# Low parts of 24 weight tiles stored in the first half of a decoder block and loaded again in the second

## The chip, the cores and the metric

One Trainium2 chip, one core of it. The metric is the device time of one execution in microseconds (us); of several runs the median is given. TensorE (PE in the profile), VectorE (DVE), ScalarE (ACT), GpSimd (POOL) and SyncE (SP) each run their own instructions in order; SP, ACT and POOL also issue DMAs.

## The reference

A decoder block on x (1 x 1024 x 1024, float32), one layer. Cut to what matters here:

```python
h = modulate(rms_norm(x, norm1_w), shift1, scale1)
proj = einsum('btd,de->bte', h, w_in)              # 1024 x 7184
q, k, v, r, a_lr, su, sv, g_a, g_b = split(proj)
...                                                # gated linear attention on q, k, v; spatial gating on su, sv
merged = sigmoid(g_a) * o_gla + sigmoid(g_b) * o_sgu
x = x + gate1 * einsum('bte,ed->btd', merged, w_out)
h2 = modulate(rms_norm(x, norm2_w), shift2, scale2)
x = x + gate2 * peer(h2, peer_w_q, keys1, keys2, expert_down, expert_up)   # top-16 product keys, gathered experts
out = rms_norm(x, final_norm_w)
```

The three large products (w_in, w_out, peer_w_q) are dense; `peer` picks 128 experts for each token out of 16384 and gathers their rows.

## The kernel before

**Halves.** The 1024 tokens are worked on in two halves of 512 (`hf` 0 and 1). In each half the activations lie transposed in on-chip memory, and all dense products of the block are made for this half, so every weight is read from DRAM once in each half.

**High and low parts.** A float32 product is made of three matmuls in the fast format `F32R`: each operand is split into a high part, which is the value rounded to that format, and a low part, which is what remains. The products high x high, high x low and low x high are summed in PSUM (`mm3`, `mm3s`, lines 175 to 189). `hTh` and `hTl` are the two parts of the activations, `wh` and `wl` those of a weight tile.

**Weight tiles.** A tile is 128 x 512 float32, 256 KB. `plan` lists the tiles of both halves in the order of use: in each half 14 groups of `w_inp` with 8 tiles each (`order_`: V0, V1, QK0, QK1, SV0, SV1, R0, ...), 32 tiles of `w_outp` and 40 of `w_qp`, 184 in all, so 368 in the program. `weights_ahead(n)` takes tiles from the plan until n are made: SP issues the load into `wt` (4 buffers, `WT`; L1250), ScalarE copies it to `wh` (L1253), VectorE subtracts `wl = wt - wh` (L1254); `wh` and `wl` have 4 buffers each (`WS`). `stream` calls it with `LOOK + 1`, so that three tiles beyond the one in use are made. `group` multiplies one group's 8 tiles with the 512 tokens, 12 matmuls per tile, into four PSUM banks, and then an `ev_...` function empties them: `ev_v` on ScalarE (L1316), `ev_qk` on VectorE (L1382 to L1402) with factors that ScalarE computes.

**What else runs there.** In the first half the rows of the adaLN modulation are made from `w_ada` beside the groups (`ada_row`, loads on SP at L1103, sums on VectorE at L1106 and L1108). In the second half the best expert of each head, for the four token blocks of the first half, is worked off beside the groups (`direct_rows`): POOL gathers a row of `down` and of `up` for each token (L752, 512 KB each), VectorE forms the dot product (L764), ScalarE the GELU (L766), VectorE adds the weighted row to `yd` (L773). The routing of the first half's tokens also runs there (`route`, `pack_half`, `rare`: many small VectorE instructions; `rare` gathers scores `qsc` with an index `qix`, L422 and L428). After the attention of the second half the stream of the other experts begins (`peer_stream`), which runs to the end of the program.

**Order.** The code is traced without loops on the chip, and `TileContext(nc, schedule_with_timeline_sim=True)` then orders each engine's instructions by a planned timeline: an instruction stands where the plan has it ready, with the order of tracing as its priority. `tc.issue_after(x)` holds an instruction behind x. On the chip each engine goes through its instructions strictly in that order and waits on semaphores. A buffer of a pool is given again when all that read or write it are done; that wait falls on the instruction that writes it next.

Of the kernel before, what the change touches and what calls it, by code (L numbers as in the profile page):

```python
# [7 lines left out]
F32 = mybir.dt.float32  # L8
F32R = mybir.dt.float32r
# [3 lines left out]
OP = mybir.AluOpType  # L13
# [4 lines left out]
P = 128  # L18
D = 1024
KD = D // P  # L20
SEQ = 1024
HALF = 512
NHALF = SEQ // HALF
# [23 lines left out]
WT = 4  # L47
# [23 lines left out]
DIR = 4  # L71
RR = .5
RA = 1.0
NEG = -3.0e38
TINY = 1.1754944e-38

# [4 lines left out]
def block_kernel(ctx: ExitStack, tc: tile.TileContext, x, xT, cT, w_ada, b_ada, b_adaT, n1T, w_inp, w_alr,  # L81
                 w_al, b_alT, gla_w, ln_w, ln_b, wsT, sgu_bT, w_outp, n2_w, w_qp, keysT, tab, down, up, fin_w,
                 out, dbg=None):
    nc = tc.nc
# [3 lines left out]
    dram = ctx.enter_context(tc.tile_pool(name="dram", bufs=1, space=DRAM))  # L88
# [53 lines left out]
    s_g = [dram.tile([len(bs), P, PH * 2 * NK], F32, name=f"s_d{g}") for g, bs in enumerate(GROUPS)]  # L142
    yr_d = [dram.tile([P, D], F32, name=f"yr_d{g}") for g in range(NG)]
    y_d = [dram.tile([P, D], F32, name=f"y_d{b}") for b in range(BH)]
    ncs_of = [NCS] * NBLK + [TOPK] * NG
    tsh_d = [dram.tile([P, BH, 5 * NCS + 2], F32, name=f"tsh_d{i}") for i in range(NHALF)]
    ts_d = [tsh_d[b // BH][:, b % BH] for b in range(NBLK)]
# [55 lines left out]
    def tops16(v, ix, st):  # L203
        nc.vector.max(v[:, 0:8], st)
        nc.vector.max_index(ix[:, 0:8], v[:, 0:8], st)
        nc.vector.match_replace(st, v[:, 0:8], st, NEG)
        nc.vector.max(v[:, 8:16], st)
# [834 lines left out]
    qa, qr, qp, qdir, qm, qf = Queue(), Queue(), Queue(), Queue(), Queue(), Queue()  # L1042
    rate = {"a": 1.0, "r": RA, "d": RD, "p": RP, "m": 1.0}

# [8 lines left out]
    with ExitStack() as pa:  # L1053
        wst_p = pa.enter_context(tc.tile_pool(name="wstage", bufs=WT))
        wsp = pa.enter_context(tc.tile_pool(name="wsplit", bufs=WS))
# [184 lines left out]
        plan, made, last_wt = [], [], []  # L1240
        for _ in range(NHALF):
            plan += [(w_inp[g], k) for g in order_ for k in range(KD)]
            plan += [(w_outp[m], k) for _ in range(2) for k in range(KD) for m in range(2)]
            plan += [(w_qp[q], k) for q in (0, 0, 1, 2, 3) for k in range(KD)]

        def weights_ahead(n):
            while plan and len(made) < n:
                src, k = plan.pop(0)
                wt = wst_p.tile([P, 512], F32, name="wt")
                last_wt[:] = [nc.sync.dma_start(wt, src[:, k, :]).ins]  # L1250
                wh = wsp.tile([P, 512], F32R, name="wh")
                wl = wsp.tile([P, 512], F32R, name="wl")
                nc.scalar.activation(wh, wt, AF.Identity)  # L1253
                nc.vector.tensor_tensor(wl, wt, wh.bitcast(F32), op=OP.subtract)  # L1254
                made.append((wh, wl))

        for hf in range(NHALF):
# [6 lines left out]
            def stream(srcs, body, evac, pre=None, npsum=4, post=None):  # L1264
                pss = [mm.tile([P, 512], F32, name="mm", tag="mm") for _ in range(npsum)]
                for k in range(KD):
                    if pre:
                        pre(k)
                    weights_ahead(len(srcs) if pre else LOOK + 1)
                    ws = [made.pop(0) for _ in srcs]  # L1270
                    body(k, ws, pss)
                    if post and k in post:
                        post[k]()
                    step()
                for i in range(npsum):
                    evac(i, pss[i])
# [485 lines left out]
```

## Time and profile before

| | |
|---|---|
| median of 3 runs | 1452.01 us (1451.76 to 1453.45) |
| the profiled execution, its own time | 1450.17 us |
| its span, first to last instruction | 1448.4 us |
| mean granted TensorE clock | 0.971 |
| DMA moved, mean rate over the span | 345.00 MB, 238 GB/s |
| loads of `wt` from `w_inp` | 224, median 3.5 us from issue to landing |
| ScalarE copy `wh<-wt` | 368, mean 628 ns |
| VectorE subtract `wl<-wt,wh` | 368, mean 685 ns |

The rows of the profile that the text below shows are of these kinds. A group of instructions: line, engine, operation, output and inputs by the program's names, shape and count, then busy us and mean ns of one, then the idle time of the engine just before them and what ended it. A wait: who waited for whom, total us, times, longest. A timeline row: start in us from the span's start, duration, engine, line, operation, names, count, and in brackets the engine's idle time before it and what ended that. A stretch: its bounds and length, the busy time of each engine with the count of instructions, the granted TensorE clock, the mean share of the 16 DMA engines that were busy, and GB/s. Matmuls are pipelined, so their durations overlap: the spacing of the starts, not the duration, is what one costs.

### The profile page before, as it was taken

The page shows a single profiled execution, that of the slowest core. Times are in us where ns is not written, and L with a number is a line of the kernel's source. Part 1 is how long each engine was busy: PE and PEld are TensorE (multiplying, and loading weights), DVE is VectorE, ACT ScalarE, POOL GpSimd, SP SyncE. Part 2 cuts the span into 40 slices and gives each one's busy share as a digit, 9 for nine tenths or more (in the row PEclk, how much of TensorE's full clock was granted, in tenths as well). Part 3 has the DMA queues.
Part 4 walks back from the last instruction along what each step waited for, and adds up shares of the span by engine and source line. Part 5 has one row for each costly group of instructions (what it writes and reads, how often), then busy time and mean ns, then how long its engine had stood idle before and what let it go on. Part 6 is the DMA issues. An engine that isn't in the chain of part 4 may idle for free.

```text
span 1448.4 us, 19642 instructions
## 1 busy us (share of the span) xinstructions
PE 1348.1 (93%) x6004; PEld 1039.6 (72%) x6004; DVE 1091.7 (75%) x3114; ACT 737.9 (51%) x1611; POOL 278.7 (19%) x275
## 2 busy tenths in 40 slices
PE   3999999999999889997989999999988999789996
PEld 2778877888888778776868787887766886445553
DVE  6584768443468669988879888778889877799775
ACT  4454333333255456474534677556645555556542
POOL 0100001000000011422442133221111024443331
PEclk8899999999999999998999999999998999999999
DMA  9552454322258484757587689796687669987984
GB/s 321 184 214 95 170 184 161 105 95 88 88 171 280 160 291 168 265 177 275 194 308 263 222 325 343 286 354 216 219 324 264 227 216 356 355 347 303 419 331 166
DMA packets 120836, 345.00 MB, mean 238 GB/s; under 512 B 15033, under 2 KB 24505, under 8 KB 108690
## 3 DMA queue, kind: packets, MB, share of 16 engines
q0 software_dynamic: 32064, 165.95, 30.7%
q1 hardware_dynamic: 70992, 133.20, 26.8%
q10 hardware_dynamic: 17666, 44.53, 8.5%
q8 instruction: 48, 0.79, 0.2%
q14 instruction: 66, 0.54, 0.1%
HBM read 319.40 MB, written 24.23 MB: 237 GB/s over the span
## 4 chain that ended last, share of the span: by engine, by line
PE 41%; DMA 8%; DVE 7%; issue 5%; ACT 4%; POOL 1%; ACTq 0%; DVEq 0%; POOLq 0%
PE acc L606 7%; PE mm L181 6%; PE mm L182 6%; PE mm L184 6%; DMA uv<-in_tab_dram,ix 4%; PE mm L187 3%; PE mm L188 3%; PE mm L189 3%; PE aux L1655 2%; PE hps L578 1%; DMA wt<-in_w_inp_dram 1%; PE hps L579 1%; DVE wl L1254 1%; DVE uv L580 1%; DMA xb<-in_x_dram 1%
## 5 line engine op out<-in xcount | busy, mean ns | idle before, releaser
L1253 ACT ACTIVATE wh<-wt 128x512 fp32r<-128x512 f32 x368 | 228.2, 628 | 322.9 <-PE mm L182 133.5
L1254 DVE TENSOR_TENSOR wl<-wt,wh 128x512 fp32r<-128x512 f32 x368 | 247.7, 685 | 137.1 <-ACT wh L1253 73.2
L181 PE MATMUL mm<-wh,hTh 128*128 128x512 f32 x672 | 265.9, 398 | 3.1 <-ACT wh L1253 3.1
L182 PE MATMUL mm<-wh,hTl 128*128 128x512 f32 x672 | 263.8, 395 | 0.0
L184 PE MATMUL mm<-wl,hTh 128*128 128x512 f32 x672 | 207.6, 394 | 0.0
L181 PEld LDWEIGHTS mm<-wh,hTh 128*128 128x128 f32 x672 | 127.1, 189 | 35.0 <-ACT wh L1253 4.8
L182 PEld LDWEIGHTS mm<-wh,hTl 128*128 128x128 f32 x672 | 126.9, 189 | 27.1 <-issue 1.0
L184 PEld LDWEIGHTS mm<-wl,hTh 128*128 128x128 f32 x672 | 125.6, 188 | 27.0 <-DVE wl L1254 0.6
L525 POOL DMA_INDIRECT uv<-in_tab_dram,ix x74 | 80.4, 1086 | 262.9 <-ACT ix L557 178.3
L187 PE MATMUL mm<-wh,hTh 128*128 128x512 f32 x224 | 90.5, 413 | 8.4 <-ACT hTh L1211 5.5
L182 PE MATMUL mm<-hTl,wh 128*128 128x512 f32 x240 | 96.5, 402 | 0.0
L181 PE MATMUL mm<-hTh,wh 128*128 128x512 f32 x240 | 95.9, 400 | 0.0
L580 DVE SCALAR_TENSOR_TENSOR uv<-uv,hps 128x512 f32<-128x512 f32 x112 | 74.8, 679 | 24.5 <-DMA uv<-in_tab_dram,ix 16.8
L188 PE MATMUL mm<-wl,hTh 128*128 128x512 f32 x224 | 89.1, 398 | 0.1
L189 PE MATMUL mm<-wh,hTl 128*128 128x512 f32 x224 | 88.4, 397 | 0.0
L187 PE MATMUL mm<-hTh,wh 128*128 128x256 f32 (+1 forms) x208 | 71.6, 346 | 10.7 <-DVE q L1383 7.6
L188 PE MATMUL mm<-hTl,wh 128*128 128x256 f32 (+1 forms) x208 | 69.8, 337 | 3.0 <-DVE hTl L173 3.0
L184 PE MATMUL mm<-hTh,wl 128*128 128x512 f32 x240 | 71.4, 398 | 0.0
L752 POOL DMA_INDIRECT uvd<-in_down_dram,dix x32 | 37.1, 1159 | 177.8 <-DVE cidx L353 40.0
L618 DVE SCALAR_TENSOR_TENSOR vl<-uv,r,vh 128x512 fp32r<-128x512 f32 x84 | 61.3, 745 | 10.6 <-ACT vh L617 7.7
L189 PE MATMUL mm<-hTh,wl 128*128 128x256 f32 (+1 forms) x208 | 68.9, 337 | 0.0
L578 PE MATMUL hps<-hh,E 128*128 128x512 f32 x132 | 62.4, 473 | 4.5 <-DVE uv L580 3.6
(938 smaller groups left out, 2875.3 us busy)
## 6 DMA issues: line engine op xcount, KB each, us to landing
wt<-in_w_inp_dram SPq DMA_DIRECT2D x224, 256.0 KB, 3.5
wt<-in_w_qp_dram SPq DMA_DIRECT2D x80, 256.0 KB, 3.0
wada<-in_w_ada_dram SPq DMA_DIRECT2D x32, 512.0 KB, 4.8
wt<-in_w_outp_dram SPq DMA_DIRECT2D x64, 256.0 KB, 3.5
wada<-in_w_ada_dram SPq DMA_DIRECT2D x32, 256.0 KB, 5.8
s_d<-so ACTq DMA_DIRECT2D x28, 256.0 KB, 5.3
xr<-in_x_dram ACTq DMA_DIRECT2D x8, 512.0 KB, 6.5
x_d<-x ACTq DMA_DIRECT2D x8, 512.0 KB, 4.4
```

What stands on the lines that cost most here:

```text
L181: nc.tensor.matmul(ps, lh, rh, start=False, stop=False)
L182: nc.tensor.matmul(ps, *((lh, rl) if feat else (ll, rh)), start=False, stop=False)
L184: nc.tensor.matmul(ps, *((ll, rh) if feat else (lh, rl)), start=False, stop=False)
L187: nc.tensor.matmul(ps, lh, rh, start=first, stop=False)
L188: nc.tensor.matmul(ps, lh, rl, start=False, stop=False)
L189: return nc.tensor.matmul(ps, ll, rh, start=False, stop=last).ins
L525: nc.gpsimd.indirect_dma_start(out=dst[:], out_offset=None, in_=src, in_offset=off)
L578: nc.tensor.matmul(hps, Ej, hh[:, sl], start=True, stop=False)
L580: nc.vector.scalar_tensor_tensor(uv[0][:, sl], uv[0][:, sl], 1.0, hps, op0=OP.mult, op1=OP.mult, accum_out=r[:, 2 + n:3 + n])
L606: ins = nc.tensor.matmul(acc[:, sl], W, v[:, sl], start=first, stop=last).ins
L1253: nc.scalar.activation(wh, wt, AF.Identity)
L1254: nc.vector.tensor_tensor(wl, wt, wh.bitcast(F32), op=OP.subtract)
```

## The change

For the groups at places 1, 2 and 3 of the order (`KEEP`: V1, QK0, QK1, 24 tiles) the first half stores each low part to DRAM on SP's queue, after VectorE has made it. In the second half, VectorE makes no low part for these 24 tiles; SP loads it from DRAM straight into the `wl` buffer. `wh` is made by ScalarE in both halves as before. `wl` gets five buffers (`WL`). While tiles of the first half are left in the plan, `wt` is loaded one tile at a time as before; from then on up to three `wt` loads (`WT - 1`) are traced ahead of the copy and the subtract or load of the first of them. Nothing else is changed, and the numbers computed are the same.

```diff
+KEEP = (1, 2, 3)
+WL = 5
...
+    wl_d = [dram.tile([P, 512], F32, name=f"wl_d{i}") for i in range(len(KEEP) * KD)]
...
+        keeps = [KEEP.index(i // KD) * KD + i % KD if i // KD in KEEP else None
+                 for i in (n % (len(plan) // NHALF) for n in range(len(plan)))]
+        staged, kept_wl, late_plan = [], set(), len(plan) // NHALF
+
         def weights_ahead(n):
-            while plan and len(made) < n:
-                src, k = plan.pop(0)
-                wt = wst_p.tile([P, 512], F32, name="wt")
-                last_wt[:] = [nc.sync.dma_start(wt, src[:, k, :]).ins]
+            while (plan or staged) and len(made) < n:
+                while plan and len(staged) < (1 if len(plan) > late_plan else WT - 1):
+                    src, k = plan.pop(0)
+                    wt = wst_p.tile([P, 512], F32, name="wt")
+                    last_wt[:] = [nc.sync.dma_start(wt, src[:, k, :]).ins]
+                    staged.append(wt)
+                wt, keep = staged.pop(0), keeps.pop(0)
                 wh = wsp.tile([P, 512], F32R, name="wh")
-                wl = wsp.tile([P, 512], F32R, name="wl")
+                wl = wsp.tile([P, 512], F32R, name="wl", bufs=WL)
                 nc.scalar.activation(wh, wt, AF.Identity)
-                nc.vector.tensor_tensor(wl, wt, wh.bitcast(F32), op=OP.subtract)
+                if keep in kept_wl:
+                    nc.sync.dma_start(wl.bitcast(F32), wl_d[keep])
+                else:
+                    nc.vector.tensor_tensor(wl, wt, wh.bitcast(F32), op=OP.subtract)
+                    if keep is not None:
+                        nc.sync.dma_start(wl_d[keep], wl.bitcast(F32))
+                        kept_wl.add(keep)
                 made.append((wh, wl))
```

## The prediction

> **What bounds the kernel now.** I read the totals of the page first, then the busy time by stage, and last the waits of the stages that the change touches. The span is 1448.4 us and the profiled execution took 1450.17 us, so 1.8 us lie around the span; the median of the runs, 1452.01 us, is 1.8 us above that execution. I make the sum against the execution and carry the difference over to the median. About 0.2% (2.9 us) is what a measurement of this kernel can tell from no change.
>
> ```profile
> span 1448.4 us, 19642 instructions
> PE 1348.1 (93%) x6004; PEld 1039.6 (72%) x6004; DVE 1091.7 (75%) x3114; ACT 737.9 (51%) x1611; POOL 278.7 (19%) x275
> L1254 DVE TENSOR_TENSOR wl<-wt,wh 128x512 fp32r<-128x512 f32 x368 | 247.7, 685 | 137.1 <-ACT wh L1253 73.2
> ```
>
> TensorE is the bound, busy for 93%. The change takes 24 of the 368 subtracts away. Counting the subtracts in order, the tiles of V1, QK0 and QK1 are the 9th to 32nd in the first half (about 45 to 137 us) and the 193rd to 216th in the second. The two rows here are the first and the last of the second 24 (the last is the second of the pair).
>
> ```profile
> 599.25 0.69 DVE L1254 TENSOR_TENSOR wl<-wt,wh 128x512 fp32r<-128x512 f32 x1
> ...
> 683.05 1.29 DVE L1254 TENSOR_TENSOR wl<-wt,wh 128x512 fp32r<-128x512 f32 x2
> ```
>
> The busy time by stretch (columns: stretch, its length, then busy us and count of PE, PEld, DVE, ACT, POOL; granted clock, DMA share, GB/s):
>
> ```profile
> core 0: us, PE busy (x) PEld busy (x) DVE busy (x) ACT busy (x) POOL busy (x), PEclk, DMA share, GB/s
> 45.00:137.00 92.00, 92.00 (x416) 71.14 (x415) 60.11 (x93) 45.89 (x77) 3.74 (x10) 0.99 0.45 164
> 595.00:640.00 45.00, 43.73 (x187) 32.65 (x187) 37.56 (x137) 27.78 (x58) 12.57 (x12) 1.00 0.59 206
> 640.00:658.00 18.00, 18.00 (x80) 14.64 (x78) 14.48 (x34) 8.16 (x17) 12.09 (x10) 1.00 0.81 283
> 658.00:666.00 8.00, 0.42 (x2) 0.37 (x2) 8.00 (x24) 3.08 (x6) 2.92 (x3) 0.67 1.00 392
> 666.00:690.00 24.00, 24.00 (x107) 19.87 (x107) 23.59 (x80) 13.79 (x26) 3.12 (x4) 0.90 0.56 190
> 690.00:760.00 70.00, 63.90 (x303) 52.62 (x302) 54.44 (x113) 29.71 (x83) 29.55 (x27) 0.98 0.74 254
> ```
>
> Two things are to be seen. In the first half's stretch TensorE never stops, and VectorE, SP and the DMA have room. In the second half's stretch VectorE is busy for 83.6 of 95 us (37.56 + 14.48 + 8.00 + 23.59), yet TensorE loses time at two places only, and neither is a wait for a low part. What TensorE waited for between 595 and 690 us, and the longest such wait between 690 and 760 us:
>
> ```profile
> PE mm L187 <- DVE q L1383: 7.6, 1, 7.6
> PE mm L187 <- ACT vt L1316: 1.3, 1, 1.3
> ...
> PE gaux L1426 <- DVE rdr L767: 4.5, 1, 4.5
> ```
>
> So at most 7.6 + 1.3 us stand in the stretch itself and 4.5 us behind it. The 7.6 us are QK1's first matmul, which waits for a PSUM bank that VectorE empties (L1382 and L1383) once QK0 is done. VectorE is in order, so what stands ahead of these two matters:
>
> ```profile
> 634.55 0.67 DVE L1254 TENSOR_TENSOR wl<-wt,wh 128x512 fp32r<-128x512 f32 x1
> 637.20 0.68 DVE L1254 TENSOR_TENSOR wl<-wt,wh 128x512 fp32r<-128x512 f32 x1
> 641.18 0.68 DVE L1254 TENSOR_TENSOR wl<-wt,wh 128x512 fp32r<-128x512 f32 x1
> 641.79 0.68 DVE L1392 TENSOR_TENSOR dt<-G 128x512 f32<-128x512 f32 x1
> 645.95 0.14 DVE L422 CAST qix<-qr 128x1 int32<-128x1 f32 x1
> 657.10 0.49 DVE L204 MAX8 qtv<-qsc 128x8 f32<-128x128 f32 x2 [3.19 <-DMA qsc<-s_d,qix]
> 657.67 0.69 DVE L1254 TENSOR_TENSOR wl<-wt,wh 128x512 fp32r<-128x512 f32 x1
> 661.56 0.69 DVE L1254 TENSOR_TENSOR wl<-wt,wh 128x512 fp32r<-128x512 f32 x1
> 665.10 0.42 DVE L1383 SCALAR_TENSOR_TENSOR q<-mm,eG 128x256 f32<-128x256 f32 x1
> ...
> 648.41 1.44 POOL L428 DMA_INDIRECT qsc<-s_d,qix  x1 [0.30 <-issue]
> ...
> 657.70 0.39 PE L189 MATMUL mm<-hTh,wl 128*128 128x512 f32 x1
> 665.66 0.77 PE L187 MATMUL mm<-hTh,wh 128*128 128x512 f32 x1 [7.58 <-DVE q L1383]
> ```
>
> VectorE stood idle for 3.19 us for a gather (qsc), whose index (qix) it had made at 645.95 and POOL issued at 648.41. Then 8.0 us of other work came before the bank was empty.
>
> **The change part by part.**
>
> First half, the 24 stores. Each adds one issue on SP and 256 KB written. The cost on SP comes from 16 issues in a row; the transfer is bounded by the score stores of the same size.
>
> ```profile
> 7.77 10.15 SPq L1122 DMA_DIRECT2D wada<-in_w_ada_dram  x16
> ...
> SPq L1250 <- DVE wl L1254: 71.0, 23, 9.0
> ...
> s_d<-so ACTq DMA_DIRECT2D x28, 256.0 KB, 5.3
> DMA to landing us min/median/max: 2.6/2.9/6.9
> ...
> ACT wh L1253 <- PE mm L182: 19.1, 11, 3.5
> ```
>
> One issue is 10.15 / 16 = 0.63 us, 24 are 15 us on SP. A store waits for its subtract, and behind it stand the next weight load and the loads of w_ada. But in 45 to 137 us SP stood 71.0 us in 23 waits for just these subtracts: a load has to wait for the subtract four tiles earlier, which frees its buffer. The store waits for the same event, so it adds 0.63 us to the load behind it and no wait of its own. Those loads land in 2.9 us (median), and what ScalarE's copies waited for was TensorE (19.1 us), never a weight load, so the 0.63 us are covered; without that cover they would be 24 x 0.63 = 15 us. The low part's buffer is kept until its store has landed, at most some 5.3 us, while it has five tiles of 12 matmuls to go round. I take 0; the ends are -1 (five buffers) and +3 (a few late tiles).
>
> Second half, the subtracts. The subtract at 641.18 has its successor at 641.79, so one is worth 0.61 us, and 24 are 14.6 us of VectorE. Most goes nowhere, since TensorE waits for VectorE once in this stretch. At that place: three subtracts between 634 and 645.95, with no wait of VectorE between them, bring the index 1.8 us forward and with it the gather; two more behind the gather (657.67 and 661.56) bring the emptying 1.2 us forward. That is 3.0 of the 7.58 us; the gather is late next. Ends: 0 (the gather lands when it did) and 7.58.
>
> The clock after the stall is priced apart. In 658 to 666 it was granted at 0.67, and matmuls behind the stall start 0.43 us apart:
>
> ```profile
> 666.23 0.63 PE L188 MATMUL mm<-hTl,wh 128*128 128x512 f32 x1
> 666.65 0.63 PE L189 MATMUL mm<-hTh,wl 128*128 128x512 f32 x1
> ...
> 670.91 0.40 PE L182 MATMUL mm<-hTl,wh 128*128 128x512 f32 x1
> 671.15 0.40 PE L184 MATMUL mm<-hTh,wl 128*128 128x512 f32 x1
> ```
>
> From 665.66 to 670.91 there are twelve starts, which take 2.9 us at the later spacing of 0.24 us: 2.4 us lost. With 4.5 us of stall left I leave this loss as it is: 0, end -2.4. The Trainium skill ("TensorE: Matmul & The Clock Gate", The HAM clock gate) says that the clock halves after an idle window of about 3.4 us. By that page the 2.4 us would come back only when the stall falls under that; the trace agrees so far, in that the clock fell behind 7.58 us.
>
> The 4.5 us behind the stretch hang on a chain of gathered rows (direct rows). There VectorE waits for a row's transfer:
>
> ```profile
> 743.36 1.23 DVE L764 SCALAR_TENSOR_TENSOR uvd<-uvd,h2d 128x1024 f32<-128x1024 f32 x1 [2.26 <-DMA uvd<-in_down_dram,dix]
> ```
>
> A VectorE relieved of 14.6 us frees row buffers earlier, and POOL gathers earlier. Between 0 and 4.5 us I take 1.5, nearer to 0, since this row is a wait for a transfer and not for VectorE's work.
>
> The 24 loads. Each is 256 KB; at 392 GB/s (658 to 666 us) it is 0.67 us of all DMA engines. In 640 to 658 us TensorE goes through six tiles, so six loads, 4.0 us, come on top of a share of 0.81, which leaves 0.19 x 18 = 3.4 us free: 0.6 us over, and I add them to the gather. Ends 0 and 4.0. Each load waits on SP for the low part's buffer, that is for the tile five back, and stands among the weight loads of tiles ahead; those now wait for ScalarE's copy alone instead of the subtract, so they leave earlier, and the copy in turn waits for the tile four back. How long the weight loads took here to land (min, median, max):
>
> ```profile
> DMA to landing us min/median/max: 2.6/3.3/9.0
> ```
>
> A tile is 12 matmuls; at 80 in the 18 us from 640 to 658 that is 2.7 us. A low part has four tiles, 10.8 us, to land, against 9.0 us at the longest, so it is not late. I take 0 for the waits on SP, ends -1 and +2. The loads' issues, 24 x 0.63 us, fit in SP's waits.
>
> The 1.3 us wait is ScalarE's, and no instruction of ScalarE goes: 0. The staging of three loads and the fifth buffer for the rest of the second half: 0, since nothing is taken from or put on TensorE there.
>
> The sum: -3.0 - 1.5 + 0.6 = -3.9 us. What TensorE gains at 666 us it carries to the end, since in 40 slices of 36 us it is busy for nine tenths or nearly so in nearly all that follow the 18th:
>
> ```profile
> PE   3999999999999889997989999999988999789996
> ```
>  1450.17 - 3.9 = 1446.3 us for the profiled execution, and 1452.0 - 3.9 = 1448 us for the median.
>
> **The rivals.**
>
> A: hidden. The gather does not land earlier, as POOL is held by row gathers ahead of it; only the 1.2 us stay, the transfers eat 0.6. 1451.4 us. For it speaks that VectorE stood idle just there.
>
> B: larger gain. The stall falls so far that the clock stays up, and the rows' stall goes too: -7.6 - 2.4 - 4.5 + 0.6 = -13.9, so 1438 us at the most and some 1442 for half of the part beyond my sum. For it: VectorE is busy for 83.6 of the 95 us, and is what TensorE waited for. Against: the idle gather.
>
> C: slower, by transfers. In 640 to 666 us the DMA is at 0.81 and then 1.00. If the loads delay the gather and the next weight loads in full instead of filling free time, six loads in front and two in the full stretch make 8 x 0.67 = 5.4 us, against 3.0 saved, and the rows at 690 to 760 us (0.74 share) lose 2 us more instead of gaining: +4.4, 1456 us. It decides from some 4.5 us of added delay. The Trainium skill ("DMA: Bandwidth & Descriptors", Issuing engines are not separate DMA queues) says that DMAs of SP, ACT and GpSimd run on the same 16 engines and interleave; by that page the new loads do delay the gathers. The shares near 1.00 agree with it.
>
> D: another order. The program is ordered by a planned timeline (`schedule_with_timeline_sim=True`), so the engines' orders are drawn anew, in the peer stage as well, where TensorE has waits of its own, the longest this one:
>
> ```profile
> PE acc L606 <- ACT rd L536: 6.9, 1, 6.9
> ```
>
> One such wait more or less than now, beside my sum, gives 1455 or 1441 us. Nothing in the profile says which.
>
> **How the numbers follow.** The bound of 0.2% lies at 1449.1 and 1454.9 us. My case (1444 to 1450 us) has 0.33, A 0.24, B 0.14, C 0.18, D 0.11. Faster: 0.31 of mine, B and 0.05 of D, 0.50. Same: A and 0.02 of mine, 0.26. Slower: C and 0.06 of D, 0.24. The range of 1440 to 1456 us leaves out the far part of B and of C, about 0.15 together; the likeliest case alone is 1444 to 1450.
>
> **What would show it.** Right: 344 subtracts; the wait of QK1's first matmul for L1383 at 3 to 6 us instead of 7.6; VectorE's busy time some 16 us lower; weight loads in the second half released by ScalarE's copy; no new wait of TensorE for a low part. Wrong: a wait of TensorE or ScalarE on a load of a low part or on `wt`, the gather landing later behind a fuller DMA, TensorE stalls in 45 to 137 us behind stores, or differences that lie in the peer stage behind 800 us.

## The result: slower by 1.0%, and where the profile after puts it

The changed kernel takes 1466.4 us (median of 20 runs) against 1452.7 us before (20 runs beside them), a ratio of 1.0096 with a 95% interval of 1.0077 to 1.0115: 14 us slower, where 4 us faster was forecast. The profiled execution of after has a span of 1464.6 us, 16.2 us more than that of before.

The totals of the page of after, the group of the subtracts, and the issues that are new:

```profile
span 1464.6 us, 19701 instructions
PE 1355.7 (93%) x6004; PEld 1042.7 (71%) x6004; DVE 1077.8 (74%) x3090; ACT 738.5 (50%) x1613; POOL 287.7 (20%) x275
...
L1267 DVE TENSOR_TENSOR wl<-wt,wh 128x512 fp32r<-128x512 f32 x344 | 231.8, 684 | 147.6 <-ACT wh L1263 141.5
...
wl_d<-wl SPq DMA_DIRECT2D x24, 256.0 KB
wl<-wl_d SPq DMA_DIRECT2D x24, 256.0 KB
```

The change does what it says: 344 subtracts instead of 368, VectorE 13.9 us less busy, 24 stores and 24 loads. The same stretches of after as were shown of before, and behind them the whole stage in which the stream of experts runs beside the groups (760 to 1210 us), first of after and then of before:

```profile
core 0: us, PE busy (x) PEld busy (x) DVE busy (x) ACT busy (x) POOL busy (x), PEclk, DMA share, GB/s
45.00:137.00 92.00, 92.00 (x421) 72.29 (x420) 60.59 (x94) 47.22 (x80) 3.84 (x10) 1.00 0.67 237
595.00:640.00 45.00, 43.88 (x186) 32.47 (x186) 33.83 (x139) 29.21 (x61) 13.54 (x15) 1.00 0.83 288
640.00:658.00 18.00, 15.83 (x70) 12.79 (x69) 13.45 (x37) 7.80 (x18) 11.63 (x8) 1.00 0.94 333
658.00:666.00 8.00, 4.94 (x16) 3.37 (x15) 8.00 (x23) 5.15 (x8) 3.75 (x2) 0.78 1.03 406
666.00:690.00 24.00, 24.00 (x112) 20.06 (x111) 16.33 (x58) 15.87 (x27) 3.36 (x4) 0.93 0.78 262
690.00:760.00 70.00, 63.81 (x291) 53.14 (x290) 53.56 (x102) 28.50 (x80) 29.96 (x26) 0.93 0.74 248
760.00:1210.00 450.00, 420.69 (x1960) 338.27 (x1959) 365.79 (x1003) 261.69 (x570) 97.66 (x87) 0.98 0.75 264
```

```profile
760.00:1210.00 450.00, 431.10 (x2024) 347.12 (x2023) 373.76 (x1025) 272.51 (x591) 98.94 (x92) 0.98 0.77 276
```

In the stretch of the kept tiles (595 to 690 us) TensorE has neither won nor lost much: busy 88.7 us against 86.2 us before. The last two rows carry the result: between 760 and 1210 us, where the source is as it was, TensorE does 64 matmuls fewer in the same 450 us (1960 against 2024) and is busy for 10.4 us less. At the same granted clock of 0.98 this is work that comes later, not work that runs slower. Added up, TensorE's waits between 760 and 1215 us are 18.3 us in before and 30.5 us in after.

What TensorE waited for, in 595 to 690 us and then in 690 to 760 us of after:

```profile
PE mm L190 <- DVE q L1399: 3.1, 2, 2.5
PE mm L192 <- DMA wl<-wl_d: 2.2, 1, 2.2
PE mm L190 <- ACT vt L1332: 0.9, 1, 0.9
...
PE gaux L1431 <- ACT ot L1445: 3.1, 2, 2.9
PE gaux L1442 <- DVE rdr L770: 2.2, 1, 2.2
```

The 7.6 us for QK1's bank have become 3.1 us, but 2.2 us of a wait for a loaded low part are new. The 4.5 us for the rows (`rdr`) have become 2.2 us, but the waits for ScalarE (`ot`), 1.5 us in before, have grown to 4.1 us, 3.1 of them in the row shown.

The start of the first matmul of a weight tile, after minus before in the two profiled executions (worked out from both traces; counted from 0, so that tile 192 is the first of the second 24 kept tiles and 216 the first behind them):

| weight tile | 192 | 216 | 240 | 288 | 336 | 367 |
|---|---|---|---|---|---|---|
| after minus before, us | -2.0 | -2.8 | +3.1 | +8.1 | +11.4 | +15.7 |

The kept stretch brought 0.8 us. All of the loss, 18.5 us, arises behind it, bit by bit. One place in it shows its kind. The planner draws the engines' orders anew. Take the longest sequence of VectorE's instructions that stands in the same order in both traces: it holds 93 to 100% of those of before in each 100 us up to 500 us, but 61 to 82% between 900 and 1200 us. ScalarE at the end of group `su` of after, where it empties the last banks into `us` (L1324), and the matmuls behind it:

```profile
949.07 1.07 ACT L1324 ACTIVATE us<-mm 128x512 f32<-128x512 f32 x2
955.50 0.20 ACT L591 ACTIVATE r<-r 128x1 f32<-128x1 f32 x1 [5.36 <-DVE uv L588]
955.70 0.20 ACT L560 ACTIVATE ix<-r 128x1 int32<-128x1 f32 x1
955.81 0.58 ACT L1324 ACTIVATE us<-mm 128x512 f32<-128x512 f32 x1
...
956.44 3.48 PE L1522 MATMUL sps<-svg,wst 128*128 128x128 f32 x16 [4.55 <-ACT us L1324]
```

and the same place of before:

```profile
946.13 0.20 ACT L588 ACTIVATE r<-r 128x1 f32<-128x1 f32 x1 [2.25 <-DVE uv L585]
946.24 0.58 ACT L1308 ACTIVATE us<-mm 128x512 f32<-128x512 f32 x1
...
945.94 2.54 PE L1506 MATMUL sps<-svg,wst 128*128 128x128 f32 x20
948.24 0.50 PE L625 MATMUL acc<-vh,e 128*128 128x512 f32 x1
```

In both, a small step of the expert stream (`r`) stands ahead of an emptying on ScalarE and waits for VectorE's `uv`. In before it waits 2.25 us, and TensorE has matmuls to go on with. In after it waits 5.36 us, and TensorE stands still for 4.55 us. No line of these was edited.

### The profile page after: what moved, and what is told of

Its sections match the earlier page's. It is cut to its first block, busy times and chain, and to the rows that moved or that the text cites. A ratio compares the mean times of both kernels' runs of the same rounds, so it can differ in the third digit from the quotient of the medians.

```text
span 1464.6 us, 19701 instructions
## 1 busy us (share of the span) xinstructions
PE 1355.7 (93%) x6004; PEld 1042.7 (71%) x6004; DVE 1077.8 (74%) x3090; ACT 738.5 (50%) x1613; POOL 287.7 (20%) x275
## 5 line engine op out<-in xcount | busy, mean ns | idle before, releaser
L1267 DVE TENSOR_TENSOR wl<-wt,wh 128x512 fp32r<-128x512 f32 x344 | 231.8, 684 | 147.6 <-ACT wh L1263 141.5
L184 PE MATMUL mm<-wh,hTh 128*128 128x512 f32 x672 | 265.2, 397 | 3.3 <-ACT wh L1263 3.3
L184 PEld LDWEIGHTS mm<-wh,hTh 128*128 128x128 f32 x672 | 126.8, 189 | 34.2 <-ACT wh L1263 5.3
L184 PE MATMUL mm<-hTh,wh 128*128 128x512 f32 x240 | 96.2, 401 | 0.0
```

What stands on the lines that cost most here:

```text
L184: nc.tensor.matmul(ps, lh, rh, start=False, stop=False)
```

## The experiments

The theory after this reading (theory 1 below): the loss is the order drawn by the plan, set off by the fifth buffer or by something else of the change. The rivals: the staged loads (theory 2), or the traffic of the stores and loads (theory 3), cost it directly.

**One part at a time.** First, the changed kernel without the staging:

```diff
-                while plan and len(staged) < (1 if len(plan) > late_plan else WT - 1):
+                while plan and len(staged) < (1):
```

> The changed kernel, but in the second half a weight load is again traced one tile at a time (stores, loads and the fifth buffer stay). Theory 1 (the planned order of the peer stage was drawn anew, and this drawing costs the time there; no single part of the change costs it): the time is another draw, somewhere between 1445 and 1470 us, and TensorE's progress differs from the kernel before's chiefly behind 760 us. Theory 2 (the loads traced ahead cost it, since they bring weight loads forward in the peer stage against the gathers): the loss is gone, 1448 to 1453 us. Theory 3 (the transfers of the stores and loads cost it): 1463 to 1470 us as in the changed kernel.

Measured: 1462.9 us, ratio 1.0080 (1.0050 to 1.0111). The loss stays; TensorE's and VectorE's orders are those of after. The staging isn't needed for it; theories 1 and 3 are not told apart by this run.

Then the staging alone, with no tile stored or loaded and four buffers (`KEEP = ()`, `bufs=WS`):

> The kernel before with one part of the change: in the second half up to three weight loads are traced ahead; no store, no load of a low part, four buffers. Theory 1: another draw, 1445 to 1470 us, with any loss behind 760 us. Theory 2: 1463 to 1470 us. Theory 3: the time of the kernel before, 1450 to 1455 us.

Measured: 1450.7 us, 0.9991 (0.9967 to 1.0014). The order is that of before, and so is the time.

Then the fifth buffer alone, with no staging and no tile stored or loaded:

```diff
-                wl = wsp.tile([P, 512], F32R, name="wl")
+                wl = wsp.tile([P, 512], F32R, name="wl", bufs=5)
```

> The kernel before with one part of the change: five buffers for the low part; no store, no load of a low part, no loads traced ahead. The fifth buffer is of little use to the engines, since the high part has four. Theory 1: another draw wherever the order comes out different, 1445 to 1470 us; the time of before if the order stays. Theories 2 and 3: the time of the kernel before, 1450 to 1455 us.

Measured: 1463.0 us, 1.0078 (1.0059 to 1.0098). This one number brings most of the loss, without a byte of new traffic and with all 368 subtracts in place. Its order departs from that of before at a few places early on and widely from some 560 us on, and between 700 and 1000 us it is the order of after.

Then the stores alone (stored in the first half, subtracted again in the second, four buffers, no staging):

> The kernel before with one part of the change: the 24 stores of the first half, while the second half makes its low parts by the subtract as before (four buffers, nothing traced ahead). Theory 1: the first half's progress differs by under 5 us, and the total is another draw, 1445 to 1470 us. Theory 2: 1450 to 1455 us. Theory 3: some of the loss, all of it before 200 us.

Measured: 1453.1 us, 1.0001 (0.9978 to 1.0024), in the order of before (a few early instructions aside). Twenty-four stores cost nothing that can be measured.

**Order apart from what sets it off.** A buffer more and another order came together so far. The next kernels take them apart: each engine's instructions are tied one behind the other, without a wait on the chip, in an order that is recorded from another kernel's plan. What is traced last (`peer_rest`) stays free.

```diff
+    for eng, packed in ORDER.items():
+        at = ...                                     # a recorded order of this engine
+        for a, b in zip(at, at[1:]):
+            tc.add_manual_dep(traced[eng][b], traced[eng][a].name, no_sync, reason="order")
```

Five buffers, all five engines in the order of before:

> The kernel before with five buffers for the low part, and every instruction of the five engines held in the order of the kernel before (edges of order only, no waits on completion). Theory 1 (the order that the plan draws with five buffers costs the time): 1449 to 1455 us, the loss of the fifth buffer alone (1463 us) is gone. Rival 4 (the fifth buffer itself costs it, by moving other tiles' addresses or by letting subtracts start earlier on the chip): 1461 to 1466 us.

Measured: 1454.2 us, 0.9994 (0.9971 to 1.0017). The fifth buffer costs nothing by itself, and neither does tying the order.

The kernel of before, with four buffers, in the order that was planned for five:

> The reverse: the kernel before with its four buffers, and every instruction of the five engines held in the order that the plan drew for five buffers. Theory 1: 1460 to 1468 us, the loss without the fifth buffer (a little more if a subtract now stands on VectorE ahead of a wait for its buffer). Rival 4: 1449 to 1455 us.

Measured: 1471.2 us, 1.0115 (1.0075 to 1.0155), above the 1460 to 1468 us expected. Nothing of the change is in this kernel, and it has the whole loss.

The changed kernel with TensorE, VectorE, ScalarE and GpSimd in the order of before (less the 24 subtracts; SP's order free):

> The changed kernel (stores, loads, five buffers, loads traced ahead) with TensorE, VectorE, ScalarE and GpSimd held in the order of the kernel before, less the 24 subtracts; SP is left to the plan. Theory 1: the loss is gone and what stands is the change's own worth, 1444 to 1453 us (the prediction's sum said 1448). Rival 4, or the transfers of the 24 loads as the cause: 1461 to 1468 us.

Measured: 1456.6 us, 1.0010 (0.9985 to 1.0035), above the 1444 to 1453 us expected. The loss is gone, and no gain stands in its place. This kernel shows what the change itself does. What TensorE waits for in it between 595 and 760 us, the stretches around the stall, and TensorE on its way into it:

```profile
PE gaux L1448 <- DVE rdr L776: 5.3, 1, 5.3
PE mm L196 <- DVE q L1405: 4.6, 1, 4.6
PE mm L198 <- DMA wl<-wl_d: 2.8, 1, 2.8
PE mm L196 <- ACT vt L1338: 1.3, 1, 1.3
```

```profile
640.00:658.00 18.00, 15.14 (x66) 11.88 (x64) 8.95 (x26) 5.81 (x13) 9.65 (x10) 1.00 0.99 353
658.00:666.00 8.00, 3.44 (x8) 2.79 (x9) 8.00 (x24) 3.89 (x7) 3.14 (x3) 0.70 1.04 398
...
760.00:1210.00 450.00, 428.91 (x2007) 345.94 (x2006) 371.90 (x1011) 270.56 (x586) 98.30 (x92) 0.98 0.77 273
```

```profile
651.95 0.39 PE L196 MATMUL mm<-hTh,wh 128*128 128x512 f32 x1
...
655.61 0.50 PE L198 MATMUL mm<-hTh,wl 128*128 128x512 f32 x1 [2.82 <-DMA wl<-wl_d]
...
662.56 0.77 PE L196 MATMUL mm<-hTh,wh 128*128 128x512 f32 x1 [4.60 <-DVE q L1405]
```

The wait for QK1's bank fell from 7.6 to 4.6 us, by the 3.0 us forecast, but this is not the gain that was forecast. Just ahead of it, in the last tile of QK0, TensorE waits 2.8 us for a loaded low part; it comes to the bank later by that much, and so waits less there. What counts is the time from the start of that tile to QK1's first matmul: 662.56 - 651.95 = 10.6 us here, 665.66 - 655.21 = 10.5 us in before. Nothing was won. Five traces have the order of before up to here and no load of a low part: before, the staging alone, the stores alone, five buffers in the order of before, and the last kernel of this section, whose order changes only later. In these five this time is 10.2 to 11.3 us. The gather on which the stall hangs shows where the gain went:

```profile
640.88 0.15 DVE L431 CAST qix<-qr 128x1 int32<-128x1 f32 x1
655.34 0.49 DVE L213 MAX8 qtv<-qsc 128x8 f32<-128x128 f32 x2 [4.01 <-DMA qsc<-s_d,qix]
...
644.58 0.95 POOL L437 DMA_INDIRECT qsc<-s_d,qix  x1 [0.30 <-issue]
```

This execution stands 3.3 us ahead of that of before from tile 192 on and all the way to this place (the last tile of QK0 starts at 651.95 instead of 655.21 us), so times are compared from there. VectorE made the index 11.1 us ahead of that start instead of 9.3 us, which is the 1.8 us of three subtracts that were forecast. But POOL, which works off row gathers ahead of it, issued the gather only 0.6 us earlier (7.4 us ahead instead of 6.8), and from its issue to the instruction that uses it the gather took 655.34 - 644.58 = 10.8 us, against 657.10 - 648.41 = 8.7 us before and 8.6 to 9.7 us in the five traces. So the data came 1.5 us later, not 1.8 us earlier. The two subtracts behind the gather did save 1.3 us, and the rest is the 0.15 us between 10.6 and 10.5.

The DMA engines are at 0.99 in 640 to 658 us; in the same stretch of the work, 636.74 to 654.74 us of this execution, they are at 0.93, against 0.81 to 0.84 in the five traces. The Trainium skill ("DMA: Bandwidth & Descriptors", Issuing engines are not separate DMA queues) says that transfers issued by SP, ScalarE and GpSimd share the same 16 engines; this trace agrees, as GpSimd's gather took 1.1 to 2.2 us longer beside SP's new loads. The rows' wait of 5.3 us lies within what the five traces show without the change (4.5 to 5.3 us). And between 760 and 1210 us TensorE is back at 2007 matmuls.

**Is it five buffers?** The changed kernel with four buffers, in the order that its own plan draws:

```diff
-                wl = wsp.tile([P, 512], F32R, name="wl", bufs=WL)
+                wl = wsp.tile([P, 512], F32R, name="wl", bufs=WS)
```

> The changed kernel with four buffers for the low part instead of five (stores, loads and loads traced ahead stay). The plan draws an order of its own for it. Theory 1: a draw between 1444 and 1465 us; where it falls tells nothing of the loads by itself. Rival 4: 1444 to 1453 us, since the fifth buffer is gone. The transfers as the cause: 1461 to 1468 us.

Measured: 1468.9 us, 1.0123 (1.0077 to 1.0169). This is above the 1444 to 1465 us of theory 1, and nearer to the 1461 to 1468 us that stood for the transfers. Against the transfers speaks the kernel before this one, which has the same loads and no loss. So the fifth buffer is one way to the loss and not the only one: the order here is a third one, with four buffers, and it loses in the same stage (TensorE's starts against before are at -0.3 us at tile 216, and at +12.5 us at tile 367). That its loss too is the order alone was not tried by tying it.

**Where in the order.** The order planned for five buffers was cut at the 233rd subtract (some 774 us on the chip) and joined to that of before, in the kernel of before with four buffers. First its part ahead of the cut, with the rest as before; then the reverse:

> The program of before with four buffers of wl; only the order is changed: every instruction traced before the 233rd subtract (tile 232, some 774 us on the chip) stands in the order that was planned for five buffers, every later one in the order of before. Theory 1 (the loss of 0.8 to 1.2% comes from how the peer stage's instructions are ordered behind 774 us): 1449 to 1457 us, ratio 0.998 to 1.003. Rival (the order of the stretch before, 560 to 774 us, delays what the peer stage starts from, and the loss only becomes visible later): 1463 to 1471 us, ratio 1.007 to 1.013. If both parts carry some of it: in between, and the shares of this run and its counterpart add up to about 1%.

Measured: 1460.1 us, 1.0036 (1.0007 to 1.0066), just above the range of theory 1.

> The counterpart: the program of before with four buffers of wl; every instruction traced before the 233rd subtract stands in the order of before, every later one in the order that was planned for five buffers. Theory 1 (the order behind 774 us costs the time): 1461 to 1471 us, ratio 1.006 to 1.013, with the loss between tiles 232 and the end. Rival (the order ahead of 774 us costs it): 1449 to 1457 us, ratio 0.998 to 1.003.

Measured: 1472.5 us, 1.0134 (1.0099 to 1.0169). The part behind 774 us carries the whole loss, a little more than expected; the part ahead of it costs some 0.4% beside the order of before. The two together make 1.7%, against 1.15% (0.75 to 1.55) for the whole order; the three intervals together are too wide to say whether they add up. The longest waits of TensorE in 760 to 1215 us of this last kernel:

```profile
PE aux L1667 <- ACT qt L1619: 5.0, 2, 2.7
PE sps L1518 <- ACT us L1320: 4.5, 1, 4.5
PE mm L199 <- DVE hTl L185: 3.2, 3, 2.8
PE mm L193 <- ACT wh L1265: 2.7, 2, 1.8
PE acc L637 <- ACT vh L629: 2.4, 3, 1.4
```

The stall at `us` is the one shown above of after, here with nothing of the change but the order. The others differ from after's: the loss is a sum of waits of 1 to 5 us, and they fall differently in each kernel. Added up between 760 and 1215 us, TensorE's waits are 18 to 22 us in the five kernels that run in the order of before throughout (before, the staging alone, the stores alone, and the two that were tied to it) and 24 to 31 us in the six that have another order behind 774 us. They are 24 us in the kernel with only its head exchanged, which comes out of another order there. In the run of the whole order (the kernel of before in the order for five buffers) the wait for `us` was down to 1.2 us and the loss was still there, so no single one of them is the cause.

## Why the prediction was wrong, step by step

- **The step that failed** is rival D, another order, in its size and its chance. It was priced at one more wait of 6.9 us, either way, with 0.11, and the step beside it set the fifth buffer to 0 "since nothing is taken from or put on TensorE there". In place of the 6.9 us the runs show 0.8 to 1.2%, 11 to 16 us between the medians, for the kernels whose whole order is another plan's (1.0078 and 1.0115 for the order of five buffers, 1.0096 for after, 1.0123 for the changed kernel with four). The text quoted `schedule_with_timeline_sim=True` and said that the orders are drawn anew in the peer stage, but then took the longest single wait as the price, where the stage is 450 us of small steps on four engines. Its last line, "differences that lie in the peer stage behind 800 us", is in the main what happened.
- **The subtracts: the work saved was right, the wait was not.** That the subtracts gone "bring the index 1.8 us forward and with it the gather" failed in its second half: in the order of before the index came 1.8 us earlier, POOL issued the gather 0.6 us earlier, as row gathers stood ahead of it, and the data came 1.5 us later. Of the 3.0 us nothing was left at QK1's first matmul. That the bank's wait shrank by just 3.0 us, to a value within the 3 to 6 us that were named, is chance: TensorE came to it 2.8 us late. In after's own order the wait is 3.1 us, but there the gather is issued at 626.7 us instead of 648.4, which is the order's doing.
- **The 24 loads: too cheap.** +0.6 us was taken, with 4.0 as the end. The gather alone took 2.1 us longer beside them than in before, and 1.1 us longer than in the slowest of the five traces. "So it is not late" failed as well: low parts were late by 2.2 us (after) and 2.8 us (in the order of before). The late one of each kernel came 11.1 and 12.6 us behind its issue, against the 9.0 us and the slack of 10.8 us that were taken from the old profile. Ahead of this stall the late low part costs nothing more, since VectorE was busy with other work until it emptied the bank; it is the sign of being wrong that the text had named.
- **The rows' stall:** -1.5 us forecast; 5.3 us in the order of before, where the five traces without the change have 4.5 to 5.3. No gain is to be seen. It waited for transfers, as the text had noticed, and nothing shows that these got faster.
- **The first half and its stores:** 0 forecast, 1.0001 measured; in after TensorE is busy for 92.00 of the 92 us with the stores, at a DMA share of 0.67 instead of 0.45.
- **The staging:** 0 forecast, 0.9991 measured.
- **The clock:** 2.4 us of loss were left as they were. In after the granted clock in 658 to 666 us is 0.78 and matmuls are still 0.43 us apart behind the stall, though the longest single wait there is 2.5 us; a shorter stall was not enough to bring the 2.4 us back:

```profile
664.20 0.63 PE L192 MATMUL mm<-hTh,wl 128*128 128x512 f32 x1
664.62 0.63 PE L184 MATMUL mm<-hTh,wh 128*128 128x512 f32 x1
```

So without the new order the change is worth what rival A said, nothing that can be measured: by A's way in part (POOL held the gather back) and by C's in part (the gather took longer beside the loads). With the order it costs 1.0%.

What stays open: why the plan, given a buffer more or 24 loads in place of subtracts, draws a worse order. What released the subtracts, in the tile view of `wl` (us of VectorE's idle time ahead of them, and times), first of before and then of after:

```profile
  ACT wh L1253: 73.2, 58
  PE mm L184: 60.4, 31
```

```profile
  ACT wh L1263: 141.5, 96
  issue: 7.2, 14
```

In before 60.4 us ended with the last matmul of the tile four back (L184), and in after no such wait stands in the list. Subtracts that the plan may put earlier get in the way of other steps of VectorE's order; that this is how the order came out worse is only argued. Nor was it tried to give one engine alone the other order. And one trace does not tell what the change does behind its stretch: against before, the tied changed kernel loses 6.7 us from tile 192 to tile 240 (802 us), where the staging alone, the stores alone and the tied fifth buffer lose at most 1.4 us. Its granted clock is 0.93 in 760 to 780 us, where theirs and that of before is 1.00.

## What to carry to other kernels

Where a planner orders the engines, a buffer more or an instruction replaced at one place can be an edit of the order far behind it: here the fifth buffer was, and the 24 stores and the staging were not. Compare the two orders before giving a difference in time to the edit, and tie the new kernel to the old order to see what the edit itself does. Price such a redraw by the stage that it reaches, not by one wait: here it was 1% and hid an edit of no effect. A load that replaces arithmetic has to land on the DMA share that it makes itself (0.81 became 0.93 in the same stretch of the work), not on the one in the old profile. And a wait that got shorter is a gain only if the engine did not lose the time just ahead of it.

## What was not expected of the hardware

A gather of 128 indices' rows took 10.8 us from issue to use, at a DMA share of 0.93, when SP's loads of 256 KB shared its stretch; without them it took 8.6 to 9.7 us in five traces, at 0.81 to 0.84. And 24 stores of 256 KB between 45 and 137 us, which raised the share there from 0.45 in before to 0.63 in the kernel with the stores alone, cost nothing that can be measured (1.0001, 0.9978 to 1.0024).
